# Aligned operand buffers and a normed first MLP entry in a two-layer encoder

## The chip, the core and the metric

The kernel runs on one core of one Trainium2 chip. The metric is the device time of one execution in microseconds (us). The core has five engines that run their own queues of instructions and wait for each other through semaphores: PE (TensorE, matmuls; PEld is its weight load), DVE (VectorE), ACT (ScalarE), POOL (GpSimd) and SP (SyncE, which here only issues DMAs). All 581 MB of weights come from HBM once, during the run.

## The reference

Two layers of a bidirectional encoder with 256 tokens and width 2048, in float32. Each layer mixes the tokens with two kinds of attention heads and then applies an MLP of width 8192. Every sub-layer is modulated by a condition vector `c`. What matters here is the end of a layer:

```python
o = concat(diff_heads, mla_heads)                 # 256 x 2048
x = x + g_a * (o @ w_o)                           # modulated by c
u = rmsnorm(x) * (1 + sc) + sh                    # sc, sh, g from c @ w_ada
x = x + g * (square(relu(u @ w_mlp_in)) @ w_mlp_out)
```

`w_ada` makes six vectors of 2048 in each layer out of `c`: shift, scale and gate of the attention, and shift, scale and gate of the MLP (groups 0 to 5). That is a matrix of 2048 x 12288 a layer, which the kernel must read too.

## The kernel before

**Arithmetic.** x lies in SBUF transposed: 16 tiles (k) of 128 rows of the width by 256 tokens. Weights and operands are split into a high and a low part in the type fp32r (`hi`, `lo` of a weight; `h`, `hid`, `ah`/`al`, `moh`/`mol` and `do` for operands), and a product is hi·xh + hi·xl + lo·xh. Line by line:

- `mac` (L182 to L184) makes the three products of one 128 x 128 weight block with 256 tokens: three matmuls of 256 columns, or 258 (below).
- `wides` (L203, L206) takes `xh` and `xl`, which lie side by side in one buffer, as one moving operand of 512 columns for `hi`, and `xh` alone, 256 columns, for `lo`. A pair of output tiles takes 16 loads of each kind, 64 matmuls.
- `rows` (L826, L828, L830) is the MLP's second matrix: `hid` is the stationary side and the weight the moving one, 512 columns. Its results are the banks `py`.
- `tokens_by_k` (L253 to L255) makes the values of the attention, in 512 columns.

**Weights.** `weights` issues one load of up to 1 MB on SP's queue (L158) into one of 5 `raw` buffers; ACT copies it to `hi` (L146) and DVE subtracts to `lo` (L147), in halves, with 4 buffers of each. Between these loads stand the 192 loads of `w_ada`, 1 MB each (L289), which use the same 5 buffers; DVE multiplies each by the condition and sums it (L297). How many there are is set by `rate`, so many per weight load; where a group is needed sooner, `ada_need` issues all that is missing at once. A sum is ordered behind the `lo` of the weight load before it.

**The end of the attention.** `w_oa` makes the first four output tiles, then `w_ob` the other twelve in six pairs (576 matmuls of 256 columns). After each pair `update` (L858) adds into x on DVE and `sumsq` adds to the sum of squares.

**The MLP's entry.** The norm needs all of x. To have no wait there, the kernel makes the first 6 tiles (`NAHEAD`) ahead of it: `ahead_part` makes x·sc in two parts for two k (`ah` on ACT, L509; `al` on DVE, L510), with two further columns for the shift that POOL fills, so that an operand has 258 columns. `ahead_step` takes a load of `w_m0` (768 KB, two k) and does 2 x 6 x 3 matmuls into 6 banks `pa`; there are 8 steps. `ahead_rest` makes the reciprocal root of the norm after two steps and the normed operands `h` (L553 to L555) during the other six. `scaled` multiplies the six banks by the norm afterwards. The same scheme opens layer 1 (`w_a1`, from the end of layer 0's MLP) and layer 1's MLP. All 8 parts of each are made while the tiles of x appear, in `w_ob`'s loop or in `turned`.

Layer 0's attention opens otherwise: `norm_then_by_k` makes `h` two k at a time, each followed by a step of matmuls into 6 banks `pk`.

**Order.** A scheduler orders each queue from the program; PE's order is written by hand in the stretches under `manual_schedule`. Engines work in order: an instruction that waits holds up all behind it.

**Memory.** Each pool is a row of buffers. `wp` holds `raw`, `hi` and `lo`, which start at multiples of 512 bytes. `up` has 40 buffers of 2064 bytes, 2080 apart from 133120 on, so they start at all multiples of 32 modulo 512; `h`, `hid`, `ah` and `al` lie there. `tp`, with other temporary tiles, starts 256 past a multiple of 512.

Of the kernel before, what the change touches and what calls it, by code (L numbers as in the profile page):

```python
# [3 lines left out]

# [13 lines left out]
P = 128  # L18
T = 256
# [75 lines left out]
LEAD = 10  # L95
WHOLE = 6
NAHEAD = 6


RATE_A0, RATE_A1, RATE_A2, RATE_K, RATE_M = 1.1, 0.5, 0.7, 0.6, 0.66  # L100
# [3 lines left out]
class Trunk:  # L104
    def __init__(self, ctx, tc, io):
        self.nc, self.tc, self.io = tc.nc, tc, io
        pool = lambda name, bufs, **k: ctx.enter_context(tc.tile_pool(name=name, bufs=bufs, **k))
        self.cp = pool("cp", 1)
        self.wp = pool("wp", 4)
        self.up = pool("up", 40)  # L110
        self.tp = pool("tp", 6)
        self.sp = pool("sp", 8)
        self.pp = pool("pp", 8, space=bass.MemoryType.PSUM)
        self.ada_todo, self.ada_here, self.rate, self.credit = [], [], 0.0, 0.0
        self.n = 0
# [160 lines left out]
    def ada_plan(self):  # L276
        self.mod, self.macc = {}, {}
        for l in range(DEPTH):
            for g in range(6):
                self.mod[l, g] = self.cp.tile([P, NK], F32, name=f"mod{l}{g}")  # L280
                self.macc[l, g] = self.cp.tile([P, NK], F32, name=f"macc{l}{g}")
# [107 lines left out]
    def bias_setup(self):  # L389
        nc, K, pos = self.nc, self.K, self.pos  # L390
        n = T + 8
        half = lambda s, dt=F32: self.flat(s, dt)[:, : 2 * T]
        ih, il, fh, fl = (half(s, dt)[:, :n] for s, dt in (("ih", I32), ("il", I32), ("fh", F32), ("fl", F32)))
        nc.vector.tensor_scalar(ih, pos, 16, None, ALU.arith_shift_right)
        nc.vector.tensor_scalar(il, pos, 0xFFFF, None, ALU.bitwise_and)
        nc.vector.tensor_copy(fh, ih)
        nc.vector.tensor_copy(fl, il)
        lh, ll = [], []
        for i in range(2):
            lsc = half("lsc")  # L400
            trep = self.vec[:, V_T + 16 * i : V_T + 16 * i + 16].unsqueeze(2).broadcast_to([P, 16, 32])
            delta = K[:, C_DELTA : C_DELTA + 32].unsqueeze(1).broadcast_to([P, 16, 32])
            nc.vector.tensor_tensor(lsc.rearrange("p (a b) -> p a b", a=16), trep, delta, ALU.mult)
            lh.append(half("lsch", F32R))
            ll.append(half("lscl", F32R))
            nc.scalar.activation(lh[i], lsc, AF.Copy)
            nc.vector.tensor_tensor(ll[i], lsc, lh[i].bitcast(F32), ALU.subtract)
        self.bias = self.cp.tile([P, HD, 2, T], F32, name="bias")
        self.bt = fh, fl, lh, ll

    def bias_part(self, a):
        nc, K = self.nc, self.K
        fh, fl, lh, ll = self.bt
        half = lambda s, dt=F32: self.flat(s, dt)[:, : 2 * T]
        r = self.u("rel")
        for t in range(2):
            j = 2 * a + t
# [74 lines left out]

    def ahead(self, l, sh, sc, src):

        return SimpleNamespace(l=l, sh=sh, sc=sc, src=src, parts=[], banks=None, r=None)

    def ahead_part(self, st, k):

        nc = self.nc
        for g in (st.sh, st.sc):  # L500
            self.ada_need(st.l, g, k + 1)
        sh, sc = self.mod[st.l, st.sh], self.mod[st.l, st.sc]
        hi, lo = (self.flat(s, F32R).rearrange("p (a b) -> p a b", a=2) for s in ("ah", "al"))
        both = sh[:, k : k + 2].unsqueeze(2).broadcast_to([P, 2, 2])
        nc.gpsimd.tensor_copy(hi[:, :, T:], both)
        nc.gpsimd.tensor_tensor(lo[:, :, T:], both, hi[:, :, T:].bitcast(F32), ALU.subtract)
        for i in range(2):
            x, c = self.x[:, k + i], sc[:, k + i : k + i + 1]
            nc.scalar.activation(hi[:, i, :T], x, AF.Copy, scale=c)  # L509
            nc.vector.scalar_tensor_tensor(lo[:, i, :T], x, c, hi[:, i, :T].bitcast(F32), ALU.mult, ALU.subtract)  # L510
            st.parts.append((hi[:, i], lo[:, i]))

    def ahead_step(self, st, p):
# [85 lines left out]
    def layer(self, l, acc, st):  # L599
# [150 lines left out]
        o = self.mo + o  # L750
        for kq in (2, 3):
            self.by_k(banks, [io["w_oa"][l, kq]], o, 4 * kq, NK)
        st = self.ahead(l, 3, 4, io["w_m0"][l])
        for m in range(0, 4, 2):
            self.update(m, banks[m // 2], g)
            acc = self.sumsq(acc, self.x[:, m : m + 2])
            self.ahead_part(st, m)
        with self.tc.manual_schedule(engines={mybir.EngineType.PE}):
            for m in range(4, NK, 2):
                self.update(m, self.pair([io["w_ob"][l, m - 4 + j] for j in range(2)], o), g)  # L760
                acc = self.sumsq(acc, self.x[:, m : m + 2])
                self.ahead_part(st, m)
            self.rate = RATE_K
            h = self.ahead_rest(st, 0, acc, 2)
            self.rate = RATE_M
            return self.mlp(l, h, st, self.mod[l, 5])

    def mlp(self, l, h, st, g):
        io = self.io
        y = [[None] * 4 for _ in range(2)]  # L770
        acc = None
        nxt = None if l == DEPTH - 1 else self.ahead(l + 1, 0, 1, io["w_a1"][0])
        for fb in range(NFB):
            hid = []
            for m in range(0 if fb else NAHEAD, NK, 2):
                pss = self.wides([io["w_m1"][l, NK * fb + m + j - NAHEAD] for j in range(2)], h)
                if m == NAHEAD and fb == 0:
                    for b in range(0, NAHEAD, 2):
                        hid += self.relu2(*self.scaled(st, b, self.t("sum")))
# [52 lines left out]
    def turned(self, c, y, g, acc, nxt=None, last=False):  # L832

        for m in range(4 * c, 4 * c + 4, 2):
# [5 lines left out]
            self.update(m, ps, g)  # L840
            acc = self.sumsq(acc, self.x[:, m : m + 2], last and m == NK - 2)
            if nxt:
                self.ahead_part(nxt, m)
        return acc

    def interleave(self, heavy, light):
# [203 lines left out]
def _layout(i):  # L1050
# [20 lines left out]
    keep = {k: [] for k in ("w_a", "w_d", "w_t", "w_a1", "w_q", "w_kr", "w_dv", "w_uq", "w_uk", "w_uv", "w_oa", "w_ob", "w_m0", "w_m1", "w_m2")}  # L1071
    for l in range(2):
        w = f["w_in"][l]
        first = np.concatenate([w[:, 3072:3840], w[:, :768]], 1)
# [20 lines left out]
        keep["w_m0"].append(_kquarters(np.ascontiguousarray(w[:, :c]), c, 2))  # L1095
# [23 lines left out]
```

## Time and profile before

| | us |
|---|---|
| three runs | 2277.11, 2277.86, 2279.04 (median 2277.86) |
| the profiled execution | 2272.99 |
| its span | 2271.2 |
| layer 0, `w_ob` and the six tiles ahead | 363 to 499.6 of the span |
| layer 0's MLP after that | 499.6 to 1184 |
| layer 1's entry (steps 1 to 7 of `w_a1`) | 1184.5 to 1226.6 |
| layer 1's MLP entry (`w_m0`) | 1534.2 to 1569.6 |

How to read a row of the timeline: start, duration, engine, line, operation, result<-inputs, shape, count, and in brackets the idle time before it and who ended it. A row of the groups has the count, then busy time in us and the mean of one in ns, then the idle time before the group. Matmuls overlap, so a matmul's duration is longer than the distance between two starts.

### The profile page before, as it was taken

The numbers are of one execution on the slowest core, as the hardware profiler recorded it, in microseconds if no ns is written. First come the engines' busy times: TensorE is split into PE (matmuls) and PEld (weight loads), VectorE is DVE, ScalarE is ACT, GpSimd is POOL, SyncE is SP. The second block draws the span as 40 slices with busy tenths as digits, with TensorE's granted clock in tenths as the row PEclk, the third lists the DMA queues.
The fourth block names the chain that finished last, engine by engine and source line by source line (L and its number), as shares of the span: only waits on it lengthen the run. The fifth ranks groups of instructions, "written<-read, shape, count | busy, mean of one in ns | idle before, by whom it ended". The sixth has DMA issues, their size and how long they took to land.

```text
span 2271.2 us, 30768 instructions
## 1 busy us (share of the span) xinstructions
PE 2178.0 (96%) x12154; PEld 1889.0 (83%) x12154; DVE 1627.9 (72%) x2166; ACT 1159.2 (51%) x1731; POOL 38.5 (2%) x59
## 2 busy tenths in 40 slices
PE   2999999789999999999999999999999999999997
PEld 1898789688888888888888888999888888888886
DVE  7889779998768778778799886667544545544555
ACT  2555654356455445446455655647545535634543
POOL 0000000100000000000200000100000000000000
PEclk9999999899999999999999999999999999999999
DMA  9988678978878878888877675555554555555551
GB/s 361 352 317 322 248 278 297 374 278 320 324 280 321 325 302 318 314 314 319 321 270 280 256 268 215 214 186 202 188 191 177 204 186 183 189 193 191 190 186 56
DMA packets 84387, 585.38 MB, mean 258 GB/s; under 512 B 9361, under 2 KB 9745, under 8 KB 17425
## 3 DMA queue, kind: packets, MB, share of 16 engines
q1 hardware_dynamic: 84242, 583.42, 68.8%
q8 instruction: 95, 1.56, 0.3%
q14 instruction: 50, 0.41, 0.0%
HBM read 581.28 MB, written 2.10 MB: 257 GB/s over the span
## 4 chain that ended last, share of the span: by engine, by line
PE 89%; DVE 7%; DMA 1%; ACT 1%; issue 1%; DVEq 0%; ACTq 0%; SPq 0%
PE ps L203 21%; PE ps L206 11%; PE py L828 10%; PE py L826 10%; PE py L830 10%; DVE ada L297 3%; PE pk L239 3%; PE ps L184 2%; PE ps L183 2%; PE ps L182 2%; DVE lo L147 1%; PE pv L255 1%; PE pv L253 1%; PE pv L254 1%; PE pa L184 1%; PE pa L183 1%
## 5 line engine op out<-in xcount | busy, mean ns | idle before, releaser
L147 DVE TENSOR_TENSOR lo<-raw,hi 128x1024 fp32r<-128x1024 f32 (+1 forms) x716 | 850.3, 1202 | 514.9 <-ACT hi L146 341.3
L146 ACT ACTIVATE hi<-raw 128x1024 fp32r<-128x1024 f32 (+1 forms) x716 | 739.9, 1040 | 700.6 <-PE py L830 393.4
L203 PE MATMUL ps<-h,hi 128*128 128x512 f32 x2112 | 503.4, 395 | 0.9 <-ACT hi L146 0.9
L203 PEld LDWEIGHTS ps<-h,hi 128*128 128x128 f32 x2112 | 392.5, 188 | 89.1 <-ACT hi L146 1.4
L297 DVE SCALAR_TENSOR_TENSOR ada<-ada,cond 128x2048 f32<-128x2048 f32 x192 | 437.7, 2286 | 7.4 <-ACT cond L343 6.9
L826 PE MATMUL py<-hi,hid 128*128 128x512 f32 x1024 | 331.3, 394 | 0.0
L828 PE MATMUL py<-lo,hid 128*128 128x512 f32 x1024 | 331.3, 394 | 0.0
L830 PE MATMUL py<-hi,hid 128*128 128x512 f32 x1024 | 330.8, 394 | 0.0
L206 PEld LDWEIGHTS ps<-h,lo 128*128 128x128 f32 x2112 | 259.2, 188 | 5.9
L206 PE MATMUL ps<-h,lo 128*128 128x256 f32 x2112 | 260.8, 281 | 0.0
L830 PEld LDWEIGHTS py<-hi,hid 128*128 128x128 f32 x1024 | 192.2, 188 | 45.5
L828 PEld LDWEIGHTS py<-lo,hid 128*128 128x128 f32 x1024 | 192.3, 188 | 45.2
L826 PEld LDWEIGHTS py<-hi,hid 128*128 128x128 f32 x1024 | 191.8, 188 | 44.4
L864 ACT ACTIVATE sum<-ps 128x256 f32<-128x256 f32 x116 | 44.4, 383 | 121.5 <-PE ps L206 121.4
L184 PE MATMUL pa<-ah,lo 128*128 128x258 f32 x288 | 83.9, 291 | 9.3 <-DVE lo L147 9.3
L239 PE MATMUL pk<-hf,w 128*128 128x256 f32 x288 | 65.4, 388 | 22.6 <-DMA w<-in_w_a 22.6
L182 PE MATMUL pa<-ah,hi 128*128 128x258 f32 x288 | 83.8, 291 | 2.5 <-ACT hi L146 2.5
L183 PE MATMUL pa<-al,hi 128*128 128x258 f32 x288 | 83.1, 288 | 0.0
L239 PEld LDWEIGHTS pk<-hf,w 128*128 128x128 f32 x288 | 56.1, 195 | 31.4 <-ACT h L554 23.3
L176 DVE TENSOR_TENSOR hid<-relu,hid 128x256 fp32r<-128x256 f32 x128 | 48.7, 422 | 46.0 <-ACT hid L175 46.0
L184 PE MATMUL ps<-moh,lo 128*128 128x256 f32 x192 | 56.6, 295 | 9.3 <-DVE lo L147 9.3
L184 PEld LDWEIGHTS pa<-ah,lo 128*128 128x128 f32 x288 | 56.1, 195 | 11.3 <-DVE lo L147 11.3
(225 smaller groups left out, 2701.3 us busy)
## 6 DMA issues: line engine op xcount, KB each, us to landing
raw<-in_w_m SPq DMA_DIRECT2D x244, 1024.0 KB, 4.8
ada<-in_w_ada SPq DMA_DIRECT2D x192, 1024.0 KB, 5.0
raw<-in_w_ob SPq DMA_DIRECT2D x24, 1024.0 KB, 5.1
raw<-in_w_dv SPq DMA_DIRECT2D x16, 1024.0 KB, 4.8
raw<-in_w_q SPq DMA_DIRECT2D x16, 1024.0 KB, 4.8
raw<-in_w_m SPq DMA_DIRECT2D x16, 768.0 KB, 4.3
w<-in_w_a SPq DMA_DIRECT2D x24, 384.0 KB, 5.4
raw<-in_w_a SPq DMA_DIRECT2D x12, 768.0 KB, 5.6
```

What stands on the lines that cost most here:

```text
L146: nc.scalar.activation(hi, v, AF.Copy)
L147: ins = nc.vector.tensor_tensor(lo, v, hi.bitcast(F32), ALU.subtract)
L182: mm(ps, hi, x[0], start=first, stop=False, skip_group_check=shared)
L183: mm(ps, hi, x[1], start=False, stop=False, skip_group_check=shared)
L184: mm(ps, lo, x[0], start=False, stop=last, skip_group_check=shared)
L203: mm(ps.rearrange("p a b -> p (a b)"), part(w, 0, k), both, start=k == 0, stop=False)
L206: mm(ps[:, 0], part(w, 1, k), x, start=False, stop=k == nk - 1)
L239: self.nc.tensor.matmul(ps, w[i][:, j * P : j * P + P], whole[i], start=first, stop=last, skip_group_check=True)
L297: ins = nc.vector.scalar_tensor_tensor(w, w, 1.0, self.cond, ALU.mult, ALU.mult, accum_out=acc[:, i : i + 1])
L826: mm(o, xh[:, tok], hi[:, part[j]], start=start, stop=False)
L828: mm(o, xh[:, tok], lo[:, part[j]], start=False, stop=False)
L830: mm(o, xl[:, tok], hi[:, part[j]], start=False, stop=stop)
```

## The change

**Pools.** The operand with shift columns (`ah`, `al`) gets a pool of its own, `ap`, with 6 buffers, which are three parts. The tiles of `up` shrink to 2048 bytes. A small pool `fp` in front holds layer 0's sums (`macc`) and shifts the rest; with that all buffers of `wp`, `up` and `tp` start at multiples of 512 bytes. The scratch memory for dynamic DMAs falls from 16384 to 2048.

```diff
-        self.cp = pool("cp", 1)
+        self.fp = pool("fp", 1)
         self.wp = pool("wp", 4)
         self.up = pool("up", 40)
         self.tp = pool("tp", 6)
+        self.cp = pool("cp", 1)
         self.sp = pool("sp", 8)
+        self.ap = pool("ap", 6)
...
-    def flat(self, name, dt=F32):
-        return self.up.tile([P, 2 * TX], dt, tag="u", name=self.name(name))
-
     def u(self, name, dt=F32):
-        return self.flat(name, dt)[:, : 2 * T].rearrange("p (a b) -> p a b", a=2)
+        return self.up.tile([P, 2, T], dt, tag="u", name=self.name(name))
...
-        hi, lo = (self.flat(s, F32R).rearrange("p (a b) -> p a b", a=2) for s in ("ah", "al"))
+        hi, lo = (self.ap.tile([P, 2, TX], F32R, tag="a", name=self.name(s)) for s in ("ah", "al"))
```

**Parts made later.** Since `ap` holds three parts, `ahead_fill` makes three of the eight as x appears, and part p + 3 after step p. This holds at layer 1's entry and at layer 1's MLP.

```diff
+    def ahead_fill(self, st, ready=0):
+
+        st.ready += ready
+        while len(st.parts) < min(st.ready, 2 * st.steps + 6):
+            self.ahead_part(st, len(st.parts))
...
                 self.mac(ps[:, :TX], w, j * P, P, st.parts[k], k == 0, k == NK - 1)
+        st.steps += 1
+        self.ahead_fill(st)
```

**Layer 0's MLP.** It no longer works ahead of the norm. `norm_then_by_k` makes its first 12 tiles (`NNORM`) from the normed `h`: 8 steps of two k, each with two loads of the new `w_n0` (768 KB) and 72 matmuls of 256 columns, into the 6 banks, which go to `relu2` without `scaled`. So 12 instead of 6 tiles are made by k, and two instead of five pairs of `wides` follow in the first block. `ahead_part`, with its calls of `ada_need` for groups 3 and 4, leaves the loop over `w_ob`. The last sum of squares there is taken alone, as two squares that go to the mean directly.

```diff
-        st = self.ahead(l, 3, 4, io["w_m0"][l])
+        st = self.ahead(l, 3, 4, io["w_m0"][0]) if l else None
...
-            self.ahead_part(st, m)
-        with self.tc.manual_schedule(engines={mybir.EngineType.PE}):
+        with self.tc.manual_schedule(engines={mybir.EngineType.PE}) if l else nullcontext():
             for m in range(4, NK, 2):
                 self.update(m, self.pair([io["w_ob"][l, m - 4 + j] for j in range(2)], o), g)
-                acc = self.sumsq(acc, self.x[:, m : m + 2])
-                self.ahead_part(st, m)
+                acc = self.sumsq(acc, self.x[:, m : m + 2], l == 0 and m == NK - 2)
+                if st:
+                    self.ahead_fill(st, 2 if m > 4 else 6)
             self.rate = RATE_K
-            h = self.ahead_rest(st, 0, acc, 2)
...
+            if st:
+                h = self.ahead_rest(st, 0, acc, 2)
+                first = NAHEAD, lambda: [self.relu2(*self.scaled(st, b, self.t("sum"))) for b in range(0, NAHEAD, 2)]
+            else:
+                h, banks = self.norm_then_by_k(l, acc, 3, 4, io["w_n0"], 3, 0)
+                first = NNORM, lambda: [self.relu2(b) for b in banks]
```

In all, matmuls of 512 columns in `wides` go from 2112 to 2016, and their halves of 256 with them; `mac` makes 3216 instead of 2640 matmuls of 256 columns and 576 instead of 864 of 258; `rows` keeps its 3072. `ah` and `al` fall from 48 to 32 each. Lines shift: `rows` stands at L841 to L845 after, `update` at L873, `ah` at L515, `h` at L561 to L563.

What moves in the queues shows at three places. The first is SP's queue in the middle of layer 0's `w_ob`; `raw` is a load of weights and `ada` one of `w_ada`. Before:

```order
L158 DMA raw_3538<-in_w_ob 128x2048
L289 DMA ada_3551<-in_w_ada 128x2048
L289 DMA ada_3607<-in_w_ada 128x2048
L158 DMA raw_3620<-in_w_ob 128x2048
L289 DMA ada_3630<-in_w_ada 128x2048
L158 DMA raw_3680<-in_w_ob 128x2048
L289 DMA ada_3691<-in_w_ada 128x2048
L289 DMA ada_3748<-in_w_ada 128x2048
L289 DMA ada_3751<-in_w_ada 128x2048
L158 DMA raw_3764<-in_w_ob 128x2048
```

The same place after the change, and the end of `w_ob` behind it:

```order
L158 DMA raw_3506<-in_w_ob 128x2048
L289 DMA ada_3519<-in_w_ada 128x2048
L158 DMA raw_3575<-in_w_ob 128x2048
L289 DMA ada_3587<-in_w_ada 128x2048
...
L158 DMA raw_3895<-in_w_ob 128x2048
L289 DMA ada_3906<-in_w_ada 128x2048
L158 DMA raw_3985<-in_w_n 128x1536
```

From the first `w_ob` load to the first of the MLP there are 12 of `w_ob` and 21 of `w_ada` before, in bursts, and 12 and 13 after, in turn. The eight that are missing come later.

The second place is DVE's queue at layer 0's MLP norm (`rstd` is its reciprocal root, `ht` and `h` the normed operand). Before:

```order
L147 TENSOR_TENSOR lo_4108<-raw_4105,hi_4107 128x768
L147 TENSOR_TENSOR lo_4112<-raw_4105,hi_4111 128x768
L297 SCALAR_TENSOR_TENSOR ada_4067,macc_84<-ada_4067,cond 128x2048
L147 TENSOR_TENSOR lo_4161<-raw_4158,hi_4160 128x768
L147 TENSOR_TENSOR lo_4165<-raw_4158,hi_4164 128x768
L490 RECIPROCAL rstd_4155<-rstd_4155 128x256
L147 TENSOR_TENSOR lo_4218<-raw_4215,hi_4217 128x768
L553 SCALAR_TENSOR_TENSOR ht_4206<-x,mod_81,rstd_4155 128x256 x2
```

After:

```order
L297 SCALAR_TENSOR_TENSOR ada_3906,macc_88<-ada_3906,cond 128x2048
L873 SCALAR_TENSOR_TENSOR x<-ps_3832,mod_83,x 128x256 x2
L311 SCALAR_TENSOR_TENSOR mod_87<-macc_88,vec 128x2
L147 TENSOR_TENSOR lo_4038<-raw_4035,hi_4037 128x768
L147 TENSOR_TENSOR lo_4042<-raw_4035,hi_4041 128x768
L490 RECIPROCAL rstd_3967<-rstd_3967 128x256
L297 SCALAR_TENSOR_TENSOR ada_3997,macc_86<-ada_3997,cond 128x2048
L561 SCALAR_TENSOR_TENSOR ht_3976<-x,mod_87,rstd_3967 128x256 x2
L561 SCALAR_TENSOR_TENSOR ht_4082<-x,mod_87,rstd_3967 128x256
L563 SCALAR_TENSOR_TENSOR h_3977<-ht_3976,mod_85,h_3977 128x256
```

Before, the weights of the steps ahead stand around the norm, and PE has these steps to do. After, the last update, the reciprocal, one sum of an `ada` load and `ht` follow each other, and PE's next matmul needs `h`.

The third is ACT's queue at the start of layer 1's MLP. Before:

```order
L477 ACTIVATE sqx_13657<-x 128x512
L509 ACTIVATE ah_13660<-x,mod_93 128x256
L146 ACTIVATE hi_13774<-raw_13772 128x768
L146 ACTIVATE hi_13778<-raw_13772 128x768
L146 ACTIVATE hi_13829<-raw_13827 128x768
L146 ACTIVATE hi_13833<-raw_13827 128x768
L489 ACTIVATE rstd_13769<-pn_13766,eps 128x256
L146 ACTIVATE hi_13893<-raw_13891 128x768
```

After:

```order
L146 ACTIVATE hi_13769<-raw_13767 128x768
L515 ACTIVATE ah_13699<-x,mod_99 128x256 x2
L146 ACTIVATE hi_13773<-raw_13767 128x768
L146 ACTIVATE hi_13832<-raw_13830 128x768
L515 ACTIVATE ah_13753<-x,mod_99 128x256 x2
L146 ACTIVATE hi_13836<-raw_13830 128x768
L489 ACTIVATE rstd_13764<-pn_13761,eps 128x256
L146 ACTIVATE hi_13904<-raw_13902 128x768
L515 ACTIVATE ah_13813<-x,mod_99 128x256 x2
```

Before, the last `ah` is made before the first weights of the MLP; after, five pairs of `ah` stand among them, each behind the step whose buffer it takes.

More of the change, by code (lines that the diff above doesn't have):

```diff
@@ L1 @@
 import math
-from contextlib import ExitStack
+from contextlib import ExitStack, nullcontext
 from types import SimpleNamespace
@@ L391, in bias_setup @@
         n = T + 8
-        half = lambda s, dt=F32: self.flat(s, dt)[:, : 2 * T]
+        half = lambda s, dt=F32: self.up.tile([P, 2 * T], dt, tag="u", name=self.name(s))
         ih, il, fh, fl = (half(s, dt)[:, :n] for s, dt in (("ih", I32), ("il", I32), ("fh", F32), ("fl", F32)))
@@ L413, in bias_part @@
         fh, fl, lh, ll = self.bt
-        half = lambda s, dt=F32: self.flat(s, dt)[:, : 2 * T]
+        half = lambda s, dt=F32: self.up.tile([P, 2 * T], dt, tag="u", name=self.name(s))
         r = self.u("rel")
@@ L774, in mlp @@
             hid = []
-            for m in range(0 if fb else NAHEAD, NK, 2):
+            for m in range(0 if fb else done, NK, 2):
                 pss = self.wides([io["w_m1"][l, NK * fb + m + j - NAHEAD] for j in range(2)], h)
-                if m == NAHEAD and fb == 0:
-                    for b in range(0, NAHEAD, 2):
-                        hid += self.relu2(*self.scaled(st, b, self.t("sum")))
+                if leave:
+                    hid += sum(leave(), [])
+                    leave = None
                 hid += self.relu2(self.joined(pss, self.t("sum")))
@@ L842, in turned @@
             if nxt:
-                self.ahead_part(nxt, m)
+                self.ahead_fill(nxt, 2)
         return acc
@@ L1094, in _layout @@
         c = NAHEAD * P
-        keep["w_m0"].append(_kquarters(np.ascontiguousarray(w[:, :c]), c, 2))
+        if l:
+            keep["w_m0"].append(_kquarters(np.ascontiguousarray(w[:, :c]), c, 2))
+        else:
+            keep["w_n0"].append(np.stack([_kquarters(np.ascontiguousarray(w[:, c * j : c * j + c]), c, 2) for j in range(2)], 1))
         keep["w_m1"].append(_ktiles(np.ascontiguousarray(w[:, c:])))
```

17 lines of the change are left out of this document (10 added, 7 removed).

## The prediction

> **What bounds the kernel now.** I read the page's busy times first, then its chain, its costliest groups, and then the stages that the diff touches.
>
> ```profile
> PE 2178.0 (96%) x12154; PEld 1889.0 (83%) x12154; DVE 1627.9 (72%) x2166; ACT 1159.2 (51%) x1731; POOL 38.5 (2%) x59
> ...
> PE 89%; DVE 7%; DMA 1%; ACT 1%; issue 1%; DVEq 0%; ACTq 0%; SPq 0%
> ...
> L203 PE MATMUL ps<-h,hi 128*128 128x512 f32 x2112 | 503.4, 395 | 0.9 <-ACT hi L146 0.9
> ...
> L826 PE MATMUL py<-hi,hid 128*128 128x512 f32 x1024 | 331.3, 394 | 0.0
> ...
> L206 PE MATMUL ps<-h,lo 128*128 128x256 f32 x2112 | 260.8, 281 | 0.0
> ```
>
> TensorE is busy 96% of the span and is 89% of the chain, so the time can fall in two ways only: matmuls follow each other more closely, or TensorE waits less. The mean of 394 ns is no price: matmuls overlap. The price is the distance from one start to the next, which the timeline gives:
>
> ```profile
> 1636.72 0.62 PE L826 MATMUL py<-hi,hid 128*128 128x512 f32 x2
> ...
> 1639.53 0.62 PE L826 MATMUL py<-hi,hid 128*128 128x512 f32 x2
> ...
> 1642.26 0.40 PE L826 MATMUL py<-hi,hid 128*128 128x512 f32 x1
> ```
>
> Each of these rows opens the 12 matmuls (3 lines, 4 each) that stream against one `hid` tile. Twelve take 2.81 us (234 ns each) for the first tile and 2.73 us (227.5) for the second, with no idle time in either. The first tile lies in `up` at 96 bytes past a multiple of 512, the second at 256 past one (addresses of the program: tiles of 2080 bytes from 133120 on). Over a whole block of the MLP the tiles mix:
>
> ```profile
> 1625.70:1714.75 89.05, 89.05 (x385) 1.00 0.55 196
> ...
> 1714.78 7.56 PE L203 MATMUL ps<-h,hi 128*128 128x512 f32 x32
> 1722.17 3.94 PE L206 MATMUL ps<-h,lo 128*128 128x256 f32 x32
> 1725.95 7.58 PE L203 MATMUL ps<-h,hi 128*128 128x512 f32 x32
> 1733.37 3.94 PE L206 MATMUL ps<-h,lo 128*128 128x256 f32 x32
> ```
>
> 384 matmuls of the output block in 89.05 us are 231.9 ns each; 32 wide ones take 7.39 and 7.42 us (231.4), 32 of 256 columns 3.78 (118.1).
>
> The stages of layer 0 that the diff rewrites, and the two entries where operands are now made later:
>
> ```profile
> 363.00:383.00 20.00, 20.00 (x171) 20.00 (x170) 20.00 (x27) 10.72 (x16) 0.00 (x0) 1.00 0.90 329
> 383.00:451.40 68.40, 53.90 (x406) 52.57 (x404) 63.57 (x78) 19.99 (x27) 8.55 (x8) 0.90 0.99 374
> 451.40:499.60 48.20, 38.71 (x293) 37.60 (x293) 43.39 (x70) 24.93 (x44) 2.73 (x2) 0.93 0.73 265
> 499.60:556.90 57.30, 56.36 (x323) 48.99 (x322) 49.58 (x68) 37.15 (x63) 0.00 (x0) 1.00 0.84 322
> 1184.50:1226.60 42.10, 39.40 (x302) 38.12 (x301) 40.21 (x66) 23.66 (x42) 0.00 (x0) 0.96 0.71 249
> 1534.20:1569.60 35.40, 35.40 (x294) 35.30 (x293) 31.22 (x54) 23.14 (x41) 0.00 (x0) 1.00 0.57 196
> ```
>
> Columns: window; its length; busy PE, weight load, DVE, ACT, POOL; granted clock; DMA share; GB/s. From 383 to 451 (`w_ob`) TensorE loses 14.5 us, with DVE 93% busy, the DMA share at 0.99 and the clock at 0.90. In the next stage (`ahead`, 288 matmuls) it loses 9.5.
>
> **Part 1, addresses.** Operands now start on multiples of 512, as weights already do. No row of before has every operand there over a whole stage. The nearest rows are the second `hid` tile (227.5; a multiple of 256) for 512 columns, and for 256 columns a place where operand and weight lie on multiples of 512:
>
> ```profile
> 146.76 0.28 PE L182 MATMUL pk<-h,hi 128*128 128x256 f32 x1
> ...
> 147.72 0.28 PE L184 MATMUL pk<-h,lo 128*128 128x256 f32 x1
> ```
>
> Eight distances in 0.96 us: 120 ns, which is 1.9 more than 118.1. Outside layer 0's rewritten stage the after kernel has 3072 + 2016 matmuls of 512 columns: from 231.7 to some 227.1 each, 5088 × −4.6 = −23.4. To these come 2016 second halves of the wide products, × +1.9 = +3.8; about 2060 others of 256 columns that were partly aligned already, × +0.9 = +1.8; and some 430 of the token products, × −2.5 = −1.1. Sum **−18.9**. Its ends: −28 where 256 columns stay at 118.1 and 512 come to 226.5; −8 where the 512s come half of the way. Below, a rival takes it as nothing and one as a loss.
>
> [...]
>
> **Part 2, layer 0's MLP entry.** Before, `ahead` makes 6 tiles from unnormed x, so the norm is hidden behind its first two steps. Its operands cost DVE and its sums are wanted early: two or three `ada` loads stand between `w_ob` loads (33 loads in the stretch; 25 after).
>
> ```profile
> L297 DVE SCALAR_TENSOR_TENSOR ada<-ada,cond 128x2048 f32<-128x2048 f32 x20 | 45.1, 2291 | 0.0
> ...
> L147 DVE TENSOR_TENSOR lo<-raw,hi 128x1024 fp32r<-128x1024 f32 x21 | 25.2, 1224 | 1.9 <-ACT hi L146 1.9
> ...
> L478 DVE TENSOR_TENSOR acc<-acc,sqx 128x512 f32<-128x512 f32 x6 | 4.2, 693 | 0.0
> ```
>
> These are groups of the stretch from 363 to 451.4; the next are single matmuls of its timeline:
>
> ```profile
> 404.83 0.58 PE L184 MATMUL ps<-moh,lo 128*128 128x256 f32 x1 [4.37 <-DVE lo L147]
> 405.21 0.41 PE L182 MATMUL ps<-moh,hi 128*128 128x256 f32 x1
> ...
> 409.05 0.32 PE L182 MATMUL ps<-moh,hi 128*128 128x256 f32 x1
> 409.21 0.28 PE L183 MATMUL ps<-mol,hi 128*128 128x256 f32 x1
> 409.32 0.28 PE L184 MATMUL ps<-moh,lo 128*128 128x256 f32 x1
> ```
>
> The 4.37 us wait is for a `lo` that stands behind such sums. After it 18 matmuls take 3.84 us (213 ns each, 405.21 to 409.05) before the distance is 110 to 120 again: a wait of this length costs nearly 2 us more. At 374 GB/s a load of 1 MB takes 2.80 us, so 33 loads want 92 us against 69 of matmuls (576 × 120 ns), and 25 want 70. That wait goes; what is late next is a near tie. DVE per pair of `w_ob` tiles: 4 × 1.22 + 2 × 2.29 + 2 × 0.48 for the update + 0.69 for the sum of squares = 11.1 us against 11.5 of matmuls (96 × 120).
>
> Now the norm stands open between `w_ob` and the first matmul of the MLP:
>
> ```profile
> L490 DVE RECIPROCAL rstd<-rstd 128x256 f32<-128x256 f32 x9 | 15.7, 1750 | 8.3 <-ACT rstd L489 8.3
> L858 DVE SCALAR_TENSOR_TENSOR x<-ps,mod,x 128x256 f32<-128x256 f32 x24 | 10.5, 481 | 6.4 <-PE ps L184 6.4
> L487 PE MATMUL pn<-acc,mean 128*128 128x256 f32 x36 | 10.6, 421 | 17.7 <-DVE acc L478 17.6
> L489 ACT ACTIVATE rstd<-pn,eps 128x256 f32<-128x256 f32 x9 | 4.3, 475 | 6.1 <-PE pn L487 6.0
> ...
> L554 ACT ACTIVATE h<-ht,mod 128x256 fp32r<-128x256 f32 x64 | 29.2, 501 | 44.0 <-DVE ht L553 43.6
> ```
>
> (Groups of the whole run.) Two updates 0.96, a square of 256 columns priced like `h` 0.50, two means 0.84, root 0.48, reciprocal 1.75, one `ada` sum of 2.29 that the order puts ahead of `ht`, `ht` 0.48, `h` 0.50: 7.8, and some 0.15 for each of eight handovers: 9 us, then about 2 for the slow clock after it. Every matmul of the next stage stands behind it; nothing covers it. Then 576 matmuls of 120 ns where DVE has per step (8.64 us of matmuls) 4 × 0.95 of `lo`, 1.2 × 2.3 of sums, 4 × 0.48 of `ht` and `h` = 8.5: tied again. Sum: 69.1 + 3 + 9 + 2 + 69.1 + 3 + two wide pairs of 11.1 = 177.4 (a pair: 7.27 + 3.84) against 20.0 + 68.4 + 48.2 + 57.3 = 193.9 before: **−16.5**. The 3s are choices: below is 0, above the 14.5 lost before in `w_ob`. Ends −23 to −4. The eight `ada` loads that leave come later, in an MLP where DVE is half idle: nothing.
>
> **Part 3, `ahead_fill`.** `ap` holds three parts, so layer 1's entries make the other five while their steps run, ACT and DVE in order. The layer-1 entry was bound by DVE (40.21 of 42.10):
>
> ```profile
> L147 DVE TENSOR_TENSOR lo<-raw,hi 128x768 fp32r<-128x768 f32 x14 | 13.0, 950 | 0.0
> ...
> L510 DVE SCALAR_TENSOR_TENSOR al<-x,mod,ah 128x256 fp32r<-128x256 f32 x4 | 1.9, 479 | 0.0
> ```
>
> It now takes up to six more `al` there, 6 × 0.48 = **+3** (0 to +6). The layer-1 MLP entry had 4.2 us of DVE free and gets ten `al` (4.8), each two steps ahead of need: **+0.5** (0 to +4). An `ah` waits for step p to release its buffer, and the `hi` of the next weights stand behind it on ACT; four weight buffers give two steps of cover, and without these a step would cost its latency (below).
>
> **Sum.** −18.9 − 16.5 + 3 + 0.5 = −31.9 on the profiled execution: 2272.99 (span 2271.2) to 2241.1. That execution lies 4.87 below the median of the runs, 2277.86; the difference taken from that gives **2246.0**.
>
> **Rivals.**
> (a) *Addresses do nothing.* For it: the wide products mix addresses and still differ little from the output block (231.4, 231.9). Against: the two `hid` tiles. −16.5 − 1.8 (1152 matmuls of layer 0 at 118.4) + 3.5 = −14.8: 2263.
> (b) *Layer 0's new order waits as much as the old.* DMA, DVE and TensorE are tied in both halves. If each half loses the 14.5 that `w_ob` lost, 2 × 11.5 more than chosen, −16.5 turns to +6.5; half of that is likelier, +11.5: 2257.5.
> (c) *`ap` serialises the entries.* If each of ten refills costs TensorE one `ah`, one `hi` and one `lo` (0.50, then 0.87 of 128 x 768 in the row below, then 0.95: 2.3), +23: 2269.
>
> ```profile
> L146 ACT ACTIVATE hi<-raw 128x768 fp32r<-128x768 f32 (+1 forms) x19 | 16.0, 869 | 9.8 <-PE pa L183 8.3 <-PE pa L184 1.4
> ```
>
> (d) *Slower.* All operands and weights on one residue bring the distance to that of the slow tile, 234 ns, in every 512-column matmul: 5088 × 2.3 = +11.7, and 4076 × 1.9 = +7.7 for 256 columns at 120. With −13 of the other parts: 2284.3. That 256 columns are slower aligned speaks for it, the second tile against. The kernel is measurably slower from a mean of 233.6 ns on (5088 × 1.9 = 9.9 = 13 − 7.7 + 4.6).
>
> **How the numbers follow.** Forecast 0.57 (own range 2232 to 2258), (a) 0.14, (b) 0.12, (c) 0.06, (d) 0.05, better than 2232 0.06. Predicted 2246; the range 2230 to 2265 leaves out (c), (d), and the best cases. A difference under 0.2% (4.6 us) can't be told from none here. Faster: forecast, (a), (b), the better ones and part of (c), less what (a) and (b) together would leave (2274): 0.87; same 0.07; slower 0.06.
>
> **What would show it.** Part 1: 384 matmuls of an output block in 87.2 us instead of 89.05, 32 wide ones in 7.27, 32 of 256 columns in 3.84. Part 2: the last `w_ob` matmul about 72 us after the first, a gap of 9 us, the first output block some 16 earlier against `w_ob`. Part 3: at layer 1's entry 45 us instead of 42.1, with `lo` or `ah` named as releaser. Output blocks at 89 us or more would fell part 1; a `w_ob` stretch over 80 us, part 2; TensorE waits for `ah`, part 3.

## The result, and the profile after

The changed kernel takes 2236.24 us (median of four runs, 2234.84 to 2239.31), the kernel before 2277.49 beside it. The ratio is 0.982 with an interval of 0.9803 to 0.9837: 41 us less. The forecast was 2246.0, and its range, 2230 to 2265, holds the result. The profiled execution takes 2236.12 (span 2234.3), 36.9 less than that of before; the forecast difference was 31.9.

The page after, the lines that answer to those of before:

```profile
PE 2157.3 (97%) x12254; PEld 1899.1 (85%) x12254; DVE 1618.6 (72%) x2141; ACT 1151.2 (52%) x1705; POOL 25.3 (1%) x43
...
PE 91%; DVE 5%; DMA 1%; issue 1%; ACT 1%; SPq 0%; DVEq 0%; ACTq 0%
...
L203 PE MATMUL ps<-h,hi 128*128 128x512 f32 x2016 | 472.9, 391 | 0.0
...
L841 PE MATMUL py<-hi,hid 128*128 128x512 f32 x1024 | 326.0, 389 | 0.0
...
L206 PE MATMUL ps<-h,lo 128*128 128x256 f32 x2016 | 252.0, 283 | 0.0
```

TensorE is still the bound (busy for 97% of the span, 91% of the chain). Its means fell by 4 to 5 ns where a matmul has 512 columns and rose by 2 where `lo` meets 256. The distance of starts says the same, in the windows over one output block and one block of wide products, and in the timeline of one wide pair:

```profile
1598.14:1685.21 87.07, 87.07 (x386) 1.00 0.56 200
1685.21:1774.09 88.88, 88.88 (x513) 1.00 0.51 183
```

```profile
1685.21 7.42 PE L203 MATMUL ps<-h,hi 128*128 128x512 f32 x32
1692.47 4.00 PE L206 MATMUL ps<-h,lo 128*128 128x256 f32 x32
1696.30 4.04 PE L203 MATMUL ps<-h,hi 128*128 128x512 f32 x17
```

384 matmuls take 87.07 us (226.7 ns each, 231.9 before), 32 wide ones 7.26 (226.9, 231.4 before), 32 with `lo` 3.83 (119.7, 118.1 before). The window of 89.05 us behind the 231.9 was a little short: from the first matmul of a block to the first of the next stage, the kernel before takes 88.99 us in layer 0 and 89.21 in layer 1 (231.7 and 232.3 ns), the changed one 87.07 in both.

The windows over layer 0's new stage (`w_ob`, the gap, the steps by k, the two wide pairs) and layer 1's two entries; the columns are those of before:

```profile
363.85:433.82 69.97, 69.97 (x582) 69.82 (x580) 63.43 (x75) 27.14 (x30) 0.00 (x0) 1.00 0.91 351
433.82:443.59 9.77, 1.56 (x7) 0.60 (x5) 8.93 (x13) 3.23 (x7) 0.00 (x0) 0.72 0.94 325
443.59:514.89 71.30, 71.30 (x576) 71.30 (x577) 59.53 (x81) 36.28 (x55) 0.00 (x0) 0.97 0.83 295
514.89:537.12 22.23, 22.23 (x130) 19.69 (x129) 20.36 (x34) 17.78 (x32) 0.00 (x0) 1.00 0.81 308
1155.16:1200.27 45.11, 40.85 (x311) 39.54 (x309) 43.33 (x73) 25.86 (x48) 10.08 (x14) 0.96 0.66 232
1506.31:1542.82 36.51, 36.03 (x295) 35.57 (x294) 33.02 (x61) 26.07 (x49) 6.09 (x10) 1.00 0.56 194
```

`w_ob` runs with no wait at all. The norm stands open for 9.77 us, and the stage after it has a granted clock of 0.97 (0.50 from 443.59 to 448.23, then 1.00) but is never idle. This is the gap on the engines in its chain:

```profile
432.81 2.29 DVE L297 SCALAR_TENSOR_TENSOR ada<-ada,cond 128x2048 f32<-128x2048 f32 x1
...
435.02 0.87 DVE L873 SCALAR_TENSOR_TENSOR x<-ps,mod,x 128x256 f32<-128x256 f32 x2
...
435.86 0.83 ACT L146 ACTIVATE hi<-raw 128x768 fp32r<-128x768 f32 x1
...
436.60 0.40 ACT L469 ACTIVATE sqa<-x 128x256 f32<-128x256 f32 x1
...
438.64 1.74 DVE L490 RECIPROCAL rstd<-rstd 128x256 f32<-128x256 f32 x1
...
440.30 2.23 DVE L297 SCALAR_TENSOR_TENSOR ada<-ada,cond 128x2048 f32<-128x2048 f32 x1
...
442.45 1.27 DVE L561 SCALAR_TENSOR_TENSOR ht<-x,mod,rstd 128x256 f32<-128x256 f32 x3
...
443.59 1.01 PE L182 MATMUL pk<-h,hi 128*128 128x256 f32 x3 [5.84 <-ACT h L562]
```

The sum of 2.23 us stands between the reciprocal and `ht`, as the order of DVE's queue showed. Another one, begun at 432.81, ended just ahead of the update at 435.02, which waited for it. And on ACT a `hi` of 0.83 us ran ahead of the second of the two squares (`sqa`).

Divided at the first matmul of each stage (an entry ends with the last matmul of its last step), the spans of the profiled executions are these (us; the last three columns are experiments described below):

| stage | before | after | old stride | layer 0 only | no layer 0 |
|---|---|---|---|---|---|
| up to `w_ob` | 362.7 | 363.9 | 364.5 | 364.8 | 366.7 |
| `w_ob` to the first output block | 194.2 | 173.3 | 171.7 | 171.1 | 183.3 |
| rest of layer 0's MLP | 627.7 | 618.0 | 628.2 | 630.1 | 617.6 |
| layer 1's entry | 42.1 | 45.1 | 45.1 | 41.8 | 45.0 |
| layer 1's attention | 239.8 | 236.9 | 237.5 | 237.0 | 238.7 |
| layer 1's `w_ob` | 67.8 | 69.1 | 68.0 | 67.9 | 69.1 |
| layer 1's MLP entry | 35.4 | 36.5 | 36.4 | 35.4 | 36.4 |
| the rest | 701.6 | 691.5 | 699.1 | 703.8 | 689.9 |

Of the 36.9 us, 20.9 come from layer 0's stage and, divided this way, 20.1 from the stages that only got other addresses, while the two entries cost 4.1. But the stages so divided do not hold the same work. Layer 1's entry holds all eight steps of `w_a1` in both kernels, and in the changed kernel nine wide matmuls of the attention stand inside it besides, ahead of the end of the last step, and one of the MLP inside the MLP's entry. The counts show it: x311 against x302, and x295 against x294. These ten are 2.3 us of work (at 226.7 ns) that only changed its stage. Without them the addresses gave 17.8 us and the entries cost 1.8. Of the experiments in the table, "old stride" has nine such matmuls in layer 1's entry, "layer 0 only" ten, "no layer 0" none.

The first stage varies by 4 us between kernels that are alike there. The attention seems to vary by 3, but with these wide matmuls counted to it, it takes 238.7 to 239.8 us in all five.

### The profile page after: what moved, and what is told of

The parts are those of the page before. It is cut to its first block, busy times and chain, and to the rows that moved or that the text cites. A ratio compares the mean times of both kernels' runs of the same rounds, so it can differ in the third digit from the quotient of the medians.

```text
span 2234.3 us, 30873 instructions
## 1 busy us (share of the span) xinstructions
PE 2157.3 (97%) x12254; PEld 1899.1 (85%) x12254; DVE 1618.6 (72%) x2141; ACT 1151.2 (52%) x1705; POOL 25.3 (1%) x43
## 4 chain that ended last, share of the span: by engine, by line
PE 91%; DVE 5%; DMA 1%; issue 1%; ACT 1%; SPq 0%; DVEq 0%; ACTq 0%
PE ps L203 21%; PE ps L206 11%; PE py L843 10%; PE py L841 10%; PE py L845 10%; PE pk L183 2%; PE ps L183 2%; PE ps L182 2%; PE ps L184 2%; PE pk L184 2%; PE pk L182 2%; PE pk L239 2%; DVE ada L297 2%; PE pv L253 1%; PE pv L254 1%; PE pv L255 1%
## 5 line engine op out<-in xcount | busy, mean ns | idle before, releaser
L203 PE MATMUL ps<-h,hi 128*128 128x512 f32 x2016 | 472.9, 391 | 0.0
L203 PEld LDWEIGHTS ps<-h,hi 128*128 128x128 f32 x2016 | 375.0, 188 | 75.8 <-DVE h L563 0.2
L841 PE MATMUL py<-hi,hid 128*128 128x512 f32 x1024 | 326.0, 389 | 0.0
L843 PE MATMUL py<-lo,hid 128*128 128x512 f32 x1024 | 326.0, 389 | 0.0
L845 PE MATMUL py<-hi,hid 128*128 128x512 f32 x1024 | 325.7, 389 | 0.0
L206 PEld LDWEIGHTS ps<-h,lo 128*128 128x128 f32 x2016 | 250.5, 192 | 5.0
L206 PE MATMUL ps<-h,lo 128*128 128x256 f32 x2016 | 252.0, 283 | 0.0
L845 PEld LDWEIGHTS py<-hi,hid 128*128 128x128 f32 x1024 | 192.2, 188 | 40.0
L841 PEld LDWEIGHTS py<-hi,hid 128*128 128x128 f32 x1024 | 191.7, 188 | 39.1
L879 ACT ACTIVATE sum<-ps 128x256 f32<-128x256 f32 x110 | 42.1, 383 | 116.4 <-PE ps L206 115.9
L182 PE MATMUL pk<-h,hi 128*128 128x256 f32 x304 | 86.6, 288 | 6.3 <-ACT h L562 6.3
L183 PE MATMUL pk<-h,hi 128*128 128x256 f32 x304 | 87.0, 287 | 0.9 <-DVE h L563 0.7
L184 PE MATMUL pk<-h,lo 128*128 128x256 f32 x304 | 86.8, 286 | 0.0
L182 PEld LDWEIGHTS pk<-h,hi 128*128 128x128 f32 x304 | 58.9, 195 | 6.9 <-ACT h L562 6.9
L183 PEld LDWEIGHTS pk<-h,hi 128*128 128x128 f32 x304 | 59.4, 195 | 1.3 <-DVE h L563 1.3
```

Of the source, the lines that this page charges most:

```text
L182: mm(ps, hi, x[0], start=first, stop=False, skip_group_check=shared)
L183: mm(ps, hi, x[1], start=False, stop=False, skip_group_check=shared)
L184: mm(ps, lo, x[0], start=False, stop=last, skip_group_check=shared)
L203: mm(ps.rearrange("p a b -> p (a b)"), part(w, 0, k), both, start=k == 0, stop=False)
L206: mm(ps[:, 0], part(w, 1, k), x, start=False, stop=k == nk - 1)
L841: mm(o, xh[:, tok], hi[:, part[j]], start=start, stop=False)
```

## The experiments

Where a ratio is given it is to the kernel before on the same chip; the changed kernel's is 0.982.

**Addresses alone.** The changed kernel with the old distance of tiles:

```diff
     def u(self, name, dt=F32):
-        return self.up.tile([P, 2, T], dt, tag="u", name=self.name(name))
+        v = self.up.tile([P, 2 * TX], dt, tag="u", name=self.name(name))
+        return v[:, : 2 * T].rearrange("p (a b) -> p a b", a=2)
...
```

> The changed kernel, but with tiles of the operand pool 2080 bytes apart again, so that they start at all multiples of 32 modulo 512; the order of instructions is that of the changed kernel on every engine. If the addresses make the matmuls follow closer, an output block of 384 matmuls goes back from 87.1 to 89.0 us, 32 wide matmuls from 7.25 to 7.4, and the whole from 2236 to about 2255 (20.1 back outside layer 0's MLP entry, some 2 gained there, where 256 columns take 118 instead of 120 ns). If addresses do nothing and the 20 us came from elsewhere (other bank or queue timing), it stays at 2236.

It took 2252.08 us, ratio 0.9896 (0.9882 to 0.9911), so 0.0076 or 17 us are lost. The windows over a block of layer 1 and over its `w_ob`:

```profile
1607.17:1695.75 88.58, 88.58 (x387) 1.00 0.56 196
1447.06:1515.05 67.99, 67.99 (x578) 1.00 0.82 297
```

A block takes 88.58 us in layer 1 and 89.24 in layer 0, while the 576 matmuls of 256 columns take 67.99 instead of 69.12. The traces of TensorE, DVE and ACT list the same instructions in the same order as after, so the addresses set the distance: some 18 us outside layer 0's stage, and 1.5 in it the other way.

**Layer 0 alone.** The kernel before with the normed entry: old pools, all parts made ahead in layer 1.

```diff
-        st = self.ahead(l, 3, 4, io["w_m0"][l])
+        st = self.ahead(l, 3, 4, io["w_m0"][0]) if l else None
...
+                h, banks = self.norm_then_by_k(l, acc, 3, 4, io["w_n0"], 3, 0)
+                first = NNORM, lambda: [self.relu2(b) for b in banks]
...
```

> The kernel before with layer 0's normed entry alone: old pools, all eight parts made ahead in layer 1. If the entry's gain is its own (no bursts of ada loads, no operands of shift columns in the w_ob loop), the stage from w_ob to the second wide pair falls by about 21 to 23 us and the whole to 2255 or 2256. If the new entry pays only because operands are aligned too (three queues are tied there), it stays above 2262.

2254.05 us, ratio 0.9906 (0.9891 to 0.9921). The stage took 171.1 us, 23.0 less than before; the others moved by up to 2.8 us, in both directions, and together took 3.7 more. The gain is the entry's own, and does not need the aligned operands.

**Layer 0's entry undone.** The changed kernel, with all three entries ahead of the norm and with `ahead_fill`:

```diff
-        st = self.ahead(l, 3, 4, io["w_m0"][0]) if l else None
+        st = self.ahead(l, 3, 4, io["w_m0"][l])
...
```

> The changed kernel with layer 0's MLP entered ahead of the norm again, its parts made three at first and then one per step. If the normed order is what gains, the time returns to about 2257 (21 lost). The rival: most of the gain is only that the early calls for ada groups 3 and 4 leave the w_ob loop; making the parts later does that as well (only three of eight are called for there), so that half is kept: about 2246.

2248.53 us, ratio 0.9882 (0.9865 to 0.9898): nearer to the rival. Windows over `w_ob`, the eight steps ahead, and five wide pairs:

```profile
366.70:436.32 69.62, 69.36 (x578) 69.16 (x577) 64.99 (x80) 29.45 (x36) 0.00 (x0) 1.00 0.93 350
436.32:493.57 57.25, 41.41 (x299) 40.06 (x298) 56.50 (x87) 26.11 (x49) 8.13 (x10) 0.85 0.87 316
493.57:549.97 56.40, 54.73 (x317) 48.20 (x316) 48.99 (x69) 37.64 (x64) 0.00 (x0) 1.00 0.83 318
```

`w_ob` falls from 88.7 to 69.6 us, as after. So it is enough for `w_ob` that five of the eight parts, with their calls for `ada` groups, leave its loop; 13 loads of `w_ada` stand there as after, where 21 stood before. But here the parts are then made among the steps, and these rise from 48.2 to 57.3 us, with DVE 99% busy; the waits of TensorE in that stretch (waiter, releaser, us in all, times, the longest) name one `lo` that came 9.5 us late:

```profile
PE pa L184 <- DVE lo L147: 14.9, 3, 9.5
```

Half of the gain is given back there. What the normed entry adds is that this work is not needed: 10 of its 21 us. No run takes the parts and their calls for loads apart, so it is not shown which of the two cost more in `w_ob`.

**Fewer parts.** Four buffers in `ap` instead of six:

```diff
-        self.ap = pool("ap", 6)
+        self.ap = pool("ap", 4)
...
-        while len(st.parts) < min(st.ready, 2 * st.steps + 6):
+        while len(st.parts) < min(st.ready, 2 * st.steps + 4):
```

> The changed kernel with 4 buffers in the pool of shift operands instead of 6: two parts made first, the next after each step. If the parts made among the steps are what costs the 4 us at layer 1's two entries, through the order on DVE and ACT and not by waiting for a buffer, one more part costs 0.5 us of DVE per entry and the time is about 2237. If the release of a buffer is what is waited for, one step of cover is too little and each of twelve refills costs 1 to 2 us: 2248 to 2260.

2237.80 us, ratio 0.9834 (0.9819 to 0.9848). Layer 1's entry takes 46.8 us (45.1), its MLP's entry 36.3 (36.5). But 14 wide matmuls stand inside the first (nine after) and none inside the second (one after); without these it is 43.6 against 43.1, and 36.3 in both. The waits in the entry, of TensorE and of ACT's `ah`, after and here in turn:

```profile
PE pa L184 <- DVE lo L147: 4.1, 3, 3.2
...
ACT ah L515 <- PE pa L183: 4.0, 4, 1.4
...
ACT ah L515 <- PE pa L184: 1.2, 1, 1.2
```

```profile
PE pa L184 <- DVE lo L147: 4.2, 4, 2.9
...
ACT ah L515 <- PE pa L183: 5.3, 5, 1.4
```

So an `ah` does wait for TensorE's step to release its buffer, some 5 us in all with three parts and with two. TensorE's own waits name `lo` alone, and hardly grow with one part less, so the buffers do not set the entry's length.

**Where the operands lie.** Three kernels with 32, 256 and 128 unused bytes ahead of the operands (the diff shows 32), and the same order of instructions:

```diff
+        self.gp = pool("gp", 1)
         self.up = pool("up", 40)
...
+        tc.nc.gpsimd.memset(self.gp.tile([P, 8], F32, name="gap"), 0.0)
...
```

> The changed kernel with 32 unused bytes ahead of the operand pool: every operand starts 32 past a multiple of 512, weights at multiples of 512 as before; the order of instructions is unchanged. If what counts is where an operand lies, all tiles take the slow distance that single tiles at such places showed before: some 233 ns for 512 columns of the output block (89.5 us a block) and the whole at 2253 or more. If only a mixture of places costs (the change of tile), uniform operands stay at 87.1 us and 2236.

> The same with 256 unused bytes. The tile at 256 past a multiple of 512 took 227.5 ns before: a block of 87.1 us and 2236, if multiples of 256 do. If the start must be a multiple of 512, about 89 and 2250.

> The changed kernel with 128 unused bytes ahead of the operand pool. Tiles 128 past a multiple of 256 were slow before, though among neighbours at other places. If the period is 256 bytes, a block takes 89 us or more and the whole about 2255. If it is 128 or less, 87.1 and 2236.

2259.86, 2236.43 and 2260.77 us, one run each. The windows over one block (and layer 1's `w_ob` behind it for 32), for 32, 256 and 128 in turn:

```profile
1609.01:1698.61 89.60, 89.60 (x387) 1.00 0.55 194
1449.56:1516.76 67.20, 67.20 (x579) 1.00 0.82 300
```

```profile
1598.48:1685.55 87.07, 87.07 (x386) 1.00 0.57 199
```

```profile
1611.33:1700.55 89.22, 89.22 (x387) 1.00 0.55 195
```

Uniform operands at 32 give 233.3 ns on the mean of the block's matmuls, slower than the mixture of before (231.7 to 232.3). 256 is as good as 512 (87.07 us a block in both); 128 is not (89.22).

**Weights moved too.** The same 32 bytes, but ahead of the weights' pool, so that both lie at 32:

> 32 unused bytes ahead of weights and operands: all of these lie 32 past a multiple of 512. If the place of the operand relative to the weight counts, 87.1 us a block and 2236 as with 0 and 0. If the address itself counts, the slow distance of the run with operands at 32: 89.5 us or more, since the weights lie badly too.

2238.96 us in one run, of which 3.4 more than after are the stretch up to `w_ob`. The window over a block:

```profile
1602.44:1689.51 87.07, 87.07 (x387) 1.00 0.57 199
```

With weights and operands both at 32 the block is as fast as at 0 and 0 (87.07 us), and with the operands alone at 32 it takes 89.60. So it is not the address alone that counts in these runs, but how the two lie to each other.

**Only `lo` moved.** The buffers of `lo` in a pool of their own behind 32 unused bytes, all others as after:

```diff
-            lo = self.wp.tile([P, half], F32R, tag="lo", name=self.name("lo"), bufs=4)
+            lo = self.lp.tile([P, half], F32R, tag="lo", name=self.name("lo"), bufs=4)
...
```

> The changed kernel with only the lo buffers of the weights 32 bytes further (operands and hi at multiples of 512, the order unchanged). If the distance between two starts is set by where the moving stream lies relative to the stationary side, each kind of matmul changes by itself: the 256-column products with lo fall from 120 to some 117 ns (32 of them 3.74 instead of 3.84 us), wide products with hi stay at 226.5, and the products of the output block that stream lo rise from 227 to 233 ns, so that a block takes about 87.9 us. If all buffers must lie alike, all kinds slow down together: 89 us a block and more than 7.3 us per 32 wide ones.

2243.24 us in one run. Its timeline at the end of a block and over two wide pairs:

```profile
1687.86 0.62 PE L846 MATMUL py<-hi,hid 128*128 128x512 f32 x2
1688.31 0.63 PE L848 MATMUL py<-lo,hid 128*128 128x512 f32 x2
1688.78 0.62 PE L850 MATMUL py<-hi,hid 128*128 128x512 f32 x2
1689.24 7.43 PE L208 MATMUL ps<-h,hi 128*128 128x512 f32 x32
1696.51 3.95 PE L211 MATMUL ps<-h,lo 128*128 128x256 f32 x32
1700.29 7.47 PE L208 MATMUL ps<-h,hi 128*128 128x512 f32 x32
```

The wide products with `hi` keep their 7.27 us, and those with `lo` fall from 3.83 to 3.78. In the block, the two pairs with `hi` take 0.45 and 0.46 us and the one with `lo` 0.47. So each kind goes by its own two operands in the wide products, but not in the block. In the block from 1600.5 the mean distances from one start to the next are 228.8 and 231.4 ns for the two lines with `hi`, whose operands lie as after (226.7), and 233.3 for the one with `lo`. A block thus takes 88.76 us, not the 87.9 expected; why the neighbours of a matmul with `lo` are slowed is not shown. And 118 ns was reached for `lo`, not 117.

**No sum in the gap.** The loads that would be summed around layer 0's norm are held back:

```diff
-        while self.credit >= 1.0 and self.ada_todo:
+        n = 0
+        while self.credit >= 1.0 and self.ada_todo and not self.hold and n < self.cap:
             self.credit -= 1.0
             self.ada_load()
+            n += 1
+        self.hold = max(0, self.hold - 1)
```

> The changed kernel with the ada loads behind the last w_ob load and the first load of the MLP held back and caught up later, one per weight load. Two sums leave the gap at layer 0's norm: one of 2.2 us between the reciprocal and ht, and one that ran 1.2 us into the last update. If the gap is the plain chain, it falls from 9.8 to 6.4 us and the whole by 3 to 4 us (to 2232.5). The rival: the gap shrinks, but the two sums come back in the matmuls behind it, where DVE was 83% busy, and the time stays within 1 us of 2236.

2233.70 us, ratio 0.9817 (0.9801 to 0.9834). The timeline of the gap:

```profile
432.63 0.88 DVE L881 SCALAR_TENSOR_TENSOR x<-ps,mod,x 128x256 f32<-128x256 f32 x2 [0.25 <-PE ps L188]
...
435.39 1.75 DVE L496 RECIPROCAL rstd<-rstd 128x256 f32<-128x256 f32 x1 [1.02 <-ACT rstd L495]
...
437.18 1.28 DVE L567 SCALAR_TENSOR_TENSOR ht<-x,mod,rstd 128x256 f32<-128x256 f32 x3
...
438.32 1.65 PE L186 MATMUL pk<-h,hi 128*128 128x256 f32 x6 [3.47 <-ACT h L568]
```

Where 9.77 us lay open after, 5.9 do here (432.43 to 438.32). Of the 3.9 less, 3.0 are the two sums and 0.9 lie between update and reciprocal, where the `hi` no longer runs between the squares. The stage takes 169.6 us, 3.7 less, and the rest of layer 0's MLP 618.0 as after: nothing comes back there. The timed intervals overlap, so the gain stands on the stage's length alone.

**Fewer sums in layer 1's entry.** Two kernels on top of that one. The first loads more in layer 0's MLP, the second loads later instead:

```diff
-RATE_A0, RATE_A1, RATE_A2, RATE_K, RATE_M = 1.1, 0.5, 0.7, 0.6, 0.66
+RATE_A0, RATE_A1, RATE_A2, RATE_K, RATE_M = 1.1, 0.5, 0.7, 0.6, 0.74
+RATE_E = 0.2
...
-            self.rate = RATE_K
+            self.rate = RATE_E
             return self.ahead_rest(nxt, 1, acc, 2), nxt
```

> The kernel with no sum in the gap, and besides: in layer 0's MLP 0.74 instead of 0.66 ada loads per weight load, in layer 1's entry 0.2 instead of 0.6. Layer 1's entry then has one or two sums instead of five or so. If the entry is bound by DVE's work (43.3 of 45.1 us busy), it falls by some 5 us to about 40, and the MLP, where DVE has room, pays nothing: 2228. The rival: the entry waits for its parts and for the norm in any case, and stays above 44: 2233.

2236.42 us, ratio 0.983 (0.9816 to 0.9843). The entry falls to 42.2 us (45.0), but no wide matmul stands inside it, and nine do in the 45.0; without these that is 43.0. Layer 0's MLP rises from 618.0 to 621.0, and waits appear in its last output block, where DVE also makes parts:

```profile
1127.73 0.50 PE L852 MATMUL py<-lo,hid 128*128 128x512 f32 x1 [1.33 <-DVE lo L149]
```

> The kernel with no sum in the gap, and besides: 0.45 ada loads per weight load in the last output block of layer 0 (0.66), 0.2 in layer 1's entry and its MLP entry (0.6), nothing earlier; so six loads come later, in layer 1's attention and MLP. If the 3 us that the higher rate of the run before cost came from more sums in the last block, and the entry is bound by DVE, the entry stays near 42 us, the MLP goes back to 618 and the whole falls to about 2230. If the six sums cost as much wherever they stand, it is again 2234 to 2236.

2234.04 us, ratio 0.9814 (0.9801 to 0.9828). The MLP is back at 617.8 and the entry stays at 42.2, again without a wide matmul. Layer 1's attention takes 1.3 more, and has the nine to do (2.0 us); its MLP entry takes 37.8 instead of 36.5. The waits of TensorE in the entry are still there:

```profile
PE pa L189 <- DVE lo L149: 3.5, 2, 2.9
```

Three sums less (two instead of five, 6.9 us of DVE) shorten the entry by 0.8 us for equal work; the other 2.0 of the 2.8 are the wide matmuls. TensorE's waits for `lo` there are 3.5 us, where they were 4.1 after. So DVE's total work is not what sets the length here: a `lo` that comes late in the order still costs, up to 2.9 us at a time. With the sums moved, the whole is the same. Neither of these two is distinguishable from the kernel without a sum in the gap.

## Why the prediction was right, point by point

- **The bound.** TensorE's distance of starts and its waits: both fell, as forecast (its busy time by 20.7 us, the rest of the span by 16.2).
- **Part 1, addresses: −18.9 forecast.** The run with the old stride gives 18 outside layer 0's stage, and so does the table with the wide matmuls put back (17.8), so the mechanism and the size were right. By kind: 512 columns −5.0 (layer 0) and −5.6 (layer 1) in the output block and −4.5 in the wide products, where −4.6 was taken for both; `lo` with 256 +1.6 (+1.9 taken). The reason given was incomplete: a multiple of 512 is not needed. 256 does, and so does 32 for all (87.07 us a block in each); what counts is the place relative to the weights. Rivals (a) and (d) fall by the runs with operands at 0, 32 and 128 (87.07, 89.60 and 89.22 us a block). One shape starts every 226.7 ns in the first and every 233.3 in the second, and 23 us of 2236 lie between 256 and 32 unused bytes (one run each). Rival (d)'s slow distance is real: it is what operands at 32 take (233.3 ns), with the weights left where they are.
- **Part 2, layer 0's entry: −16.5 forecast, −20.9 measured.** The term was mis-sized by the 3 us of waits that were taken in each half of the near tie. `w_ob` had none (69.97 us, 72.1 taken), the steps by k had none either (71.30, 74.1 taken); the gap was 9.77 (9 taken), and the slow clock after it, 0.50 for 4.64 us, cost 2.2 (2 taken). That the gap came so near is in part luck. Its terms had one `ada` sum and eight handovers of 0.15 us; without a sum or a `hi` in the chain 5.9 us passed, for which the other terms make 6.7. So those terms were 0.8 too long (no run shows the 0.15; in that chain the reciprocal starts 0.04 us after the end of the root, 434.88 + 0.47), while the second sum and the `hi`, 1.9 us, were not foreseen. Rival (b), a full loss in both halves, was wrong on both. Of the cause, the prediction named the bursts of loads and the operands together, and no run separates them: for `w_ob` itself it suffices to move five parts, with their calls, out of the loop (69.6 us). The normed entry is needed so that they do not return in the steps behind.
- **Part 3, parts made later: +3 and +0.5 forecast, +3.0 and +1.1 measured.** That the first agrees is luck: 2.0 of the 3.0 are the nine wide matmuls. For equal work the entries cost 1.0 and 0.9 more in this pair of kernels. Against the kernel with layer 0's entry alone, whose old entry takes 39.5 us without its ten wide matmuls, layer 1's costs 3.5 more, so the size stays open. That lost time shows as TensorE waiting for `lo` (2.3 us before, 4.1 after). But the sum priced six `al` at their time on DVE, on the reading that the entry was bound by DVE (40.21 of 42.10), and 6.9 us less of DVE's work shortened the entry by only 0.8. Rival (c) is wrong in its price: `ah` does wait for buffers, but no wait of TensorE is put down to it, even with two parts.
- **From the profiled execution to the median.** Of the 9.8 us between 2246.0 and 2236.2, about 4.9 are the step that carried the 4.87 us, by which the profiled execution of before lay under its median, over to the changed kernel. Its profiled execution lies at its median (2236.12, 2236.24). Nearly all of the rest is part 2.

What stays open: why the relative place of the two operands counts, why 256 columns go the other way (116.7 ns at 32, 120.0 at 0), and what the parts made later cost in layer 1's entry. The variation in the stretch up to `w_ob`, 4 us, was not followed up.

## What to carry to other kernels

Where matmuls follow each other without waits, compare the distance of starts between buffers of one shape: if it differs (here 226.7 and 233.3 ns), look at the places of the operands relative to the weights, which a pool's padding can set (here 32 bytes). Work done ahead, with the loads it calls for early, can cost more than the wait it avoids (here layer 0's stage took 194.2 us with it, 173.3 and 171.1 without); before a stage is hidden behind another, see what its preparation does to the stage that prepares it. An open chain of 6 to 10 us was cheaper here than work ahead that kept DVE at least 90% busy, and in such a chain every instruction between its links should be one that the chain needs (two sums and a `hi` were 3.9 us of 9.8). And before two stages are compared by their lengths, count their matmuls: a schedule can move work from one stage into the next (here ten wide matmuls, 2.3 us).

## What the runs showed of the hardware

- In the output blocks, matmuls of 512 columns in fp32r started every 226.7 ns where operand and weight lay 0 and 0, 256 and 0, or 32 and 32 bytes past a multiple of 512 (384 in 87.07 us). They started every 233.3 ns where the two lay 32 and 0 past one (89.60 us), and every 232.3 at 128 and 0 (89.22). These runs have identical orders of instructions.
- With 256 columns it is the other way round: layer 1's 576 matmuls of `w_ob` took 69.12 us at 0 and 0 and at 32 and 32 (120.0 ns), and 67.20 at 32 and 0 (116.7). No kernel with a whole pool moved was faster than the changed one (2236.43 to 2260.77 us against 2236.24); with `lo` alone moved, the wide products had 227.2 and 118.1 ns, but the output blocks lost more (88.76 us instead of 87.07).
- After the open gap of 9.77 us, 71.30 us passed for 576 matmuls, which took 69.12 in layer 1's `w_ob` at a granted clock of 1.00. In the first 4.64 us behind the gap the granted clock was 0.50 and a matmul started every 0.21 us; in the other 66.66 us it was 1.00. So 2.2 us came on top of the gap itself.
